# One core, hybrid attention with PEER: the program order of the attention stage written anew

## The chip, the cores and the metric

The kernel runs on one core of one Trainium2 chip. The metric is the device time of the whole program in microseconds (us); smaller is better. The engines are named as in the profile: PE (TensorE, its weight loads apart as PEld), DVE (VectorE), ACT (ScalarE), POOL (GpSimd), and SP, whose queue issues nearly all DMAs.

## The reference

One decoder layer over 512 tokens of width 1024, all in float32. Cut to what matters:

```
ada = silu(c) @ w_ada + b_ada            # six vectors: shift, scale, gate, twice
h = x*(1+scale1) + shift1
qa, ka, va, qb, kb, vb = split(h @ w_in)
oa = sliding-window attention (8 heads, 2 KV heads, window 128, ALiBi, sinks)
ob = stick-breaking attention (8 heads): A[t,s] = sigmoid(z_ts) * prod_{s<j<t}(1 - sigmoid(z_tj))
x = layer_norm(ALPHA*x + gate1 * (concat(rms(oa), rms(ob)) @ w_out))
h = x*(1+scale2) + shift2
x = layer_norm(ALPHA*x + gate2 * peer(h))  # product-key retrieval over 128*128 single-neuron experts
```

## The kernel before

The program has three stretches. The first stage (up to about 314 us) makes the modulation vectors, the projections, both attentions, the output projection and the first layer norm. The second scores the PEER keys and takes the best sixteen, the third streams all expert weights through PE. The change touches the first stage alone.

Every product of full precision is done in three matmuls: an operand is split into a rounded high part (`uhi`, `vwhi`, `hhi`, made by ACT, line 92) and the rest (`ulo`, `vwlo`, `hlo`, made by DVE or POOL, line 93). The stage is built from a few helpers that the program calls one after another:

- `proj_chunk(i, nm)`: 128 columns of the input projection (24 matmuls, line 303, into a PSUM tile `pj`). Chunks 0 to 7 are q and k of the four stick-breaking pairs, 8 is `ka`, 9 to 12 are `qa` of the four local pairs. The weights come by SP into `uraw` (two buffers).
- `proj_v(half)`: half of all V columns (96 matmuls, line 322). It needs three SBUF tiles of the tag `big`: the raw weights, their high and their low part. The tag has four buffers.
- `ada_rows(g, ...)` and `ada_cols(g)`: one of the modulation vectors. Four transfers of 1 MB (`wa`, tag `big` too) are summed by DVE in eight steps of 128x1024 (lines 170 and 172, `acc`); then PE reduces `acc` over the partitions (lines 189 and 179).
- `sb(j, q, k)`: the weights of one stick-breaking pair, two heads r after one another. For each head: scores `z` (line 367, one PSUM tile), three ACT steps (lines 370 to 372), DVE (374), POOL cuts the causal triangle (340 and 342), DVE (376, 377), the split into `sphi` and `splo`, fourteen matmuls that add the running sums (382, 384), ACT's exponential (387), and the cut once more. There is one `z`, so the next head's scores wait for this head's exponential.
- `sbv(j, w)`: the values of that pair (line 398), into the PSUM tile `oacc`, of which there is one; then `finish_o` copies it out on ACT (lines 349 and 352 or 355).
- `swa_pair(j, q, k)`: one local pair: scores `zs` (421), DVE (424 to 436), ACT's exponentials (431), transposes `pt` (451), copies `pts` (453) and values (456), into the same `oacc`. `zs` and `pt` share two PSUM buffers.

Tile names in the profile are those of the code. The code names no engine order for this stage: it is written in program order, a scheduler ahead of the run makes a fixed order for each engine from it, in which `sb` and `sbv` have high priority, and each engine then runs its own order strictly, waiting on semaphores. A tile whose buffer is still in use makes its writer wait. So the program order decides which rows stand behind which on each engine, and which transfer stands behind which on SP.

The other lines that the rows below name: 274 is the first part of chunks 0 to 3, 556 the output projection (`zm`), 521 the sums for the RMS norm, 502 the product of the output weights with `gate1`.

Of the kernel before, what the change touches and what calls it, by code (L numbers as in the profile page):

```python
# [67 lines left out]
def tile_block(ctx, tc, xr, xT, ccol, wada, bcol, brow, wqk, wv, sinks, gncol, wout,  # L68
# [73 lines left out]
    with ExitStack() as front:  # L142
# [32 lines left out]
        def ada_cols(g):  # L175
            acc = ada_acc(g)
            p = ps.tile([P, 512], F32, name="adap", tag="m", bufs=2)
            for dc in range(DC):
                T.matmul(p[:, dc:dc + 1], acc[:, dc * P:(dc + 1) * P], ones[:, 0:1], start=True, stop=True,
                         skip_group_check=True)  # L180
            V.tensor_tensor(adac[:, g * 8:g * 8 + 8], p[:, :DC], bc[:, g * 8:g * 8 + 8], op=OP.add)

        def ada_rows(g, dst, i):
            acc = ada_acc(g)
            bb = fa.tile([P, D], F32, name="bb", tag="big", bufs=BIG)
            nc.sync.dma_start(bb, brow[i:i + 1, :].to_broadcast([P, D]))
            for h in range(2):
                p = ps.tile([P, 512], F32, name="adap", tag="m", bufs=2)
                T.matmul(p, ones, acc[:, h * 512:(h + 1) * 512], start=True, stop=True)
                V.tensor_tensor(dst[:, h * 512:(h + 1) * 512], p, bb[:, h * 512:(h + 1) * 512], op=OP.add)  # L190

        def load_w_in(i):
            return load_split(wqk[i].rearrange("p (c n) -> p c n", c=DC), [P, DC, P], "u", wsp)
# [76 lines left out]
        def half_proj(i, h):  # L270
            (hi, lo), p = heads[i]
            for dc in range(*PARTS[h]):
                for n, (a, b) in enumerate(((hi, hhi), (hi, hlo), (lo, hhi))):
                    T.matmul(p, a[:, dc], b[:, dc], start=(dc == 0 and n == 0), stop=(dc == DC - 1 and n == 2))  # L274
# [19 lines left out]
        def proj_chunk(i, nm):  # L294
            if i < 4:
                half_proj(i, len(PARTS) - 1)
                p = heads[i][1]
            else:
                hi, lo = load_w_in(i)
                p = ps.tile([P, S], F32, name="pj", tag="m", bufs=2)  # L300
                for dc in range(DC):
                    for n, (a, b) in enumerate(((hi, hhi), (hi, hlo), (lo, hhi))):
                        T.matmul(p, a[:, dc], b[:, dc], start=(dc == 0 and n == 0), stop=(dc == DC - 1 and n == 2))  # L303
            o = fw.tile([P, S], F32, name=nm, tag=nm)
            A.activation(o, p, AF.Copy, scale=0.125 if nm[0] == "q" else 1.0)
            return o
# [3 lines left out]
        def proj_v(*halves):  # L310
            for half in halves:
                raw = fa.tile([P, DC, 320], F32, name="vwraw", tag="big", bufs=BIG)
                nc.sync.dma_start(raw, wv[:, half].rearrange("p (c n) -> p c n", c=DC))
                hi = fa.tile([P, DC, 320], F32R, name="vwhi", tag="big", bufs=BIG)
                lo = fa.tile([P, DC, 320], F32R, name="vwlo", tag="big", bufs=BIG)
                split(raw, hi, lo, V)
                for tb in range(TB):
                    p = ps.tile([P, S], F32, name="pj", tag="m", bufs=2)
                    t = slice(tb * P, (tb + 1) * P)
                    for dc in range(DC):  # L320
                        for n, (a, b) in enumerate(((hhi, hi), (hhi, lo), (hlo, hi))):
                            T.matmul(p[:, :320], a[:, dc, t], b[:, dc], start=(dc == 0 and n == 0),
                                     stop=(dc == DC - 1 and n == 2))
                    A.activation(vr[:, tb, half * 320:(half + 1) * 320], p[:, :320], AF.Copy)
# [136 lines left out]
        gate1 = fc.tile([P, D], F32, name="gate1")  # L461
        def sb(j, q, k):
            with tc.high_priority():
                return sb_weights(q, k)

        def sbv(j, w):
            with tc.high_priority():
                sb_values(j, w)

        w = sb(0, proj_chunk(0, "q"), proj_chunk(1, "k"))  # L470
        q0, k0 = proj_chunk(2, "q"), proj_chunk(3, "k")
        proj_v(1)
        qa = proj_chunk(9, "qa")
        ada_rows(5, gate2, 1)
        proj_v(0)
        sbv(0, w)
        w = sb(1, q0, k0)
        ada_rows(2, gate1, 0)
        q0, k0 = proj_chunk(4, "q"), proj_chunk(5, "k")
        sbv(1, w)  # L480
        ka = proj_chunk(8, "ka")
        w = sb(2, q0, k0)
        swa_pair(0, qa, ka)
        qa1 = proj_chunk(10, "qa")
        swa_pair(1, qa1, ka)
        q0, k0 = proj_chunk(6, "q"), proj_chunk(7, "k")
        ada_cols(3)
        sbv(2, w)
        ada_cols(4)
        w = sb(3, q0, k0)  # L490
        fa_cm.__exit__(None, None, None)
        fwo = front.enter_context(tc.tile_pool(name="fwo", bufs=1, side="right", reuse_waits="tile"))
        qa2 = proj_chunk(11, "qa")
        swa_pair(2, qa2, ka)
        sbv(3, w)
        qa3 = proj_chunk(12, "qa")
        wo = [None] * DC

# [678 lines left out]
```

## Time and profile before

| | us |
|---|---|
| median of 3 runs (lowest to highest) | 1596.53 (1594.99 to 1599.22) |
| the profiled execution, its own time | 1595.99 |
| its span in the trace | 1594.3 |
| PE busy | 1554.9 (98% of the span) |
| DVE busy | 1220.3 (77%) |
| ACT busy | 647.5 (41%) |
| POOL busy | 455.8 (29%) |

The span is what the trace covers; the execution's own time is 1.69 us longer. Matmuls are pipelined and their ends are modelled, so a PE shown as busy can still hide short waits.

### The profile page before, as it was taken

What the parts mean: (1) busy time and instruction counts of PE and PEld (TensorE: products, weight loads), DVE (VectorE), ACT (ScalarE), POOL (GpSimd) and SP (SyncE); (2) the same over time, 40 slices, a digit from 0 to 9 for tenths busy, and PEclk for the clock granted to TensorE, in tenths of its full rate; (3) what the DMA queues carried; (4) which work ended last, traced back from release to release, by engine and by line L of the source; (5) the groups of instructions that cost most, each with busy time, mean ns of one, the idle gap of its engine ahead of it and who ended that gap; (6) DMA issues with size and microseconds to landing.
All of it is one profiled execution on the core that took longest, in us unless ns stands there. A gap on an engine that the chain in (4) does not pass through costs nothing.

```text
span 1594.3 us, 21985 instructions
## 1 busy us (share of the span) xinstructions
PE 1554.9 (98%) x8109; PEld 1346.3 (84%) x8109; DVE 1220.3 (77%) x2351; ACT 647.5 (41%) x935; POOL 455.8 (29%) x410
## 2 busy tenths in 40 slices
PE   8999999999989999999999999999999999999996
PEld 5776767788879999899999999999999999998885
DVE  2568585589999997578777787777877777777878
ACT  2535574333355555333333333333333333333331
POOL 0002133544400000233334333333333444333100
PEclk8999898999999999999999999999999999999999
DMA  9564132222225555999888988999889998989873
GB/s 338 184 258 158 53 112 101 79 92 81 81 80 212 219 210 202 334 327 326 305 311 301 326 301 304 306 309 322 302 303 312 307 321 301 311 282 305 261 231 119
DMA packets 147356, 382.12 MB, mean 240 GB/s; under 512 B 11312, under 2 KB 68656, under 8 KB 143280
## 3 DMA queue, kind: packets, MB, share of 16 engines
q1 hardware_dynamic: 110384, 246.49, 44.6%
q0 software_dynamic: 36864, 134.23, 24.4%
q8 instruction: 63, 1.03, 0.3%
q14 instruction: 45, 0.37, 0.1%
HBM read 351.32 MB, written 29.36 MB: 239 GB/s over the span
## 4 chain that ended last, share of the span: by engine, by line
PE 79%; DVE 12%; DMA 3%; ACT 3%; issue 1%; POOL 1%; SPq 0%; DVEq 0%; ACTq 0%; POOLq 0%
PE yb L980 32%; PE ph L970 25%; PE pw L841 5%; PE ph L806 4%; PE pj L303 3%; PE zm L556 2%; DVE scr L620 1%; PE pj L274 1%; DMA wa<-in_wada_dram 1%; DVE tsi L622 1%; DVE tsi L619 1%; PE pq L647 1%; DVE tsv L621 1%; DVE tsv L618 1%; PE oacc L398 1%
## 5 line engine op out<-in xcount | busy, mean ns | idle before, releaser
L855 POOL DMA_INDIRECT gat<-in_u_rows_dram,idx x128 | 161.6, 1262 | 478.5 <-DVE hd L873 226.5
L93 DVE TENSOR_TENSOR ulo<-uraw,uhi 128x1024 fp32r<-128x1024 f32 x133 | 162.5, 1223 | 164.9 <-ACT uhi L92 160.5
L970 PE MATMUL ph<-h2hi,ulo 128*128 128x384 f32 x768 | 258.6, 337 | 0.6 <-DVE ulo L93 0.6
L970 PE MATMUL ph<-h2hi,uhi 128*128 128x384 f32 x768 | 258.2, 336 | 0.3 <-ACT uhi L92 0.3
L970 PE MATMUL ph<-h2lo,uhi 128*128 128x384 f32 x768 | 258.2, 336 | 0.0
L855 POOL DMA_INDIRECT gat<-in_v_rows_dram,idx x128 | 161.0, 1258 | 264.8 <-DVE y L883 224.1
L980 PE MATMUL yb<-vhi,ghi 128*128 128x512 f32 x654 | 203.0, 391 | 0.0
L980 PE MATMUL yb<-vhi,glo 128*128 128x512 f32 x654 | 202.9, 391 | 0.0
L980 PE MATMUL yb<-vlo,ghi 128*128 128x512 f32 x654 | 202.6, 391 | 0.0
L92 ACT ACTIVATE uhi<-uraw 128x1024 fp32r<-128x1024 f32 x155 | 162.4, 1050 | 74.6 <-PE pq L647 52.9
L883 DVE SCALAR_TENSOR_TENSOR y<-gat,cf,y 128x1024 f32<-128x1024 f32 x127 | 162.7, 1281 | 3.9 <-DMA gat<-in_v_rows_dram,idx 1.6
L873 DVE CUSTOM_DVE_ANT_0 gscr<-gat,h2row 128x1024 f32<-128x1024 f32 x128 | 156.5, 1222 | 10.6 <-DMA gat<-in_u_rows_dram,idx 7.9
L1085 ACT ACTIVATE stash<-ph 128x384 f32<-128x384 f32 x96 | 47.2, 491 | 275.1 <-PE ph L970 275.1
L970 PEld LDWEIGHTS ph<-h2lo,uhi 128*128 128x128 f32 x768 | 144.4, 188 | 4.4
L970 PEld LDWEIGHTS ph<-h2hi,uhi 128*128 128x128 f32 x768 | 144.4, 188 | 4.4 <-ACT uhi L92 0.7
L980 PEld LDWEIGHTS yb<-vlo,ghi 128*128 128x128 f32 x654 | 122.7, 188 | 27.3
L980 PEld LDWEIGHTS yb<-vhi,glo 128*128 128x128 f32 x654 | 122.8, 188 | 26.8
L970 PEld LDWEIGHTS ph<-h2hi,ulo 128*128 128x128 f32 x768 | 144.4, 188 | 1.0 <-DVE ulo L93 1.0
L980 PEld LDWEIGHTS yb<-vhi,ghi 128*128 128x128 f32 x654 | 121.8, 188 | 18.9
L93 DVE TENSOR_TENSOR vlo<-vraw,vhi 128x1024 fp32r<-128x1024 f32 x97 | 118.4, 1220 | 17.5 <-ACT vhi L92 17.4
L92 ACT ACTIVATE vhi<-vraw 128x1024 fp32r<-128x1024 f32 x97 | 102.8, 1060 | 53.6 <-issue 35.8
L947 ACT ACTIVATE ghi<-gt 128x384 fp32r<-128x384 f32 x97 | 51.0, 525 | 177.7 <-DVE gt L920 177.7
(311 smaller groups left out, 2860.1 us busy)
## 6 DMA issues: line engine op xcount, KB each, us to landing
uraw<-in_uT_dram SPq DMA_DIRECT2D x128, 512.0 KB, 5.2
vraw<-in_v_rows_dram SPq DMA_DIRECT2D x128, 512.0 KB, 5.2
w_d<-stage SPq DMA_DIRECT2D x12, 2048.0 KB, 7.3
wt<-w_d SPq DMA_DIRECT2D x32, 768.0 KB, 9.3
wa<-in_wada_dram SPq DMA_DIRECT2D x16, 1024.0 KB, 6.5
wah<-in_wada_dram SPq DMA_DIRECT2D x16, 512.0 KB, 9.4
uraw<-in_wq_dram SPq DMA_DIRECT2D x16, 512.0 KB, 3.3
uraw<-in_wqk_dram SPq DMA_DIRECT2D x11, 512.0 KB, 7.8
```

The lines of the kernel that those rows point to most:

```text
L92: A.activation(hi, src, AF.Copy)
L93: (eng or V).tensor_tensor(lo, src, hi.bitcast(F32), op=OP.subtract)
L303: T.matmul(p, a[:, dc], b[:, dc], start=(dc == 0 and n == 0), stop=(dc == DC - 1 and n == 2))
L806: T.matmul(p[:, :ND], a[:, dc], b[:, dc, P:], start=(dc == 0 and n == 0), stop=(dc == DC - 1 and n == 2))
L841: T.matmul(p[:, k * P:(k + 1) * P], oh4[:, 1, :, k], oh4[:, 2 + j, :, k], start=(j == 0), stop=(j == 1), skip_group_check=True)
L855: G.indirect_dma_start(out=t, out_offset=None, in_=rows, in_offset=bass.IndirectOffsetOnAxis(ap=idx[:, k:k + 1], axis=0))
L873: V.tensor_tensor_reduce(out=scr, in0=t, in1=h2row, scale=1.0, scalar=0.0, op0=OP.mult, op1=OP.add, accum_out=hd[:, n:n + 1])
L883: V.scalar_tensor_tensor(y0, t, cf[:, k:k + 1], y0, op0=OP.mult, op1=OP.add)
L947: A.activation(gop[i][0], gts[i], AF.Copy)
L970: T.matmul(p[:, :ND], a[:, dc], b[:, dc, P:], start=(dc == 0 and n == 0), stop=(dc == DC - 1 and n == 2))
L980: T.matmul(ybank[b][c0 // 512][:, c0 % 512:(c1 - 1) % 512 + 1], x[:, t], y[:, c0:c1], start=(i == 0 and n == 0), stop=(n == 2 and i == (NK ...
L1085: A.activation(stash[i + LOOK], p[:, :ND], AF.Gelu_apprx_tanh)
```

## The change

The calls of the attention are put in another order; nothing is computed otherwise, and no size or pool is altered. Both V halves now come directly behind the first pair's weights, the weights of stick-breaking pair j+1 directly behind the values of pair j, and the local pairs and the modulation vectors behind those.

```diff
         w = sb(0, proj_chunk(0, "q"), proj_chunk(1, "k"))
         q0, k0 = proj_chunk(2, "q"), proj_chunk(3, "k")
+        proj_v(0)
+        sbv(0, w)
+        w = sb(1, q0, k0)
         proj_v(1)
         qa = proj_chunk(9, "qa")
         ada_rows(5, gate2, 1)
-        proj_v(0)
-        sbv(0, w)
-        w = sb(1, q0, k0)
-        ada_rows(2, gate1, 0)
         q0, k0 = proj_chunk(4, "q"), proj_chunk(5, "k")
         sbv(1, w)
+        w = sb(2, q0, k0)
         ka = proj_chunk(8, "ka")
-        w = sb(2, q0, k0)
+        ada_rows(2, gate1, 0)
+        q0, k0 = proj_chunk(6, "q"), proj_chunk(7, "k")
+        sbv(2, w)
         swa_pair(0, qa, ka)
+        w = sb(3, q0, k0)
+        ada_cols(3)
         qa1 = proj_chunk(10, "qa")
+        sbv(3, w)
         swa_pair(1, qa1, ka)
-        q0, k0 = proj_chunk(6, "q"), proj_chunk(7, "k")
-        ada_cols(3)
-        sbv(2, w)
         ada_cols(4)
-        w = sb(3, q0, k0)
         fa_cm.__exit__(None, None, None)
         fwo = front.enter_context(tc.tile_pool(name="fwo", bufs=1, side="right", reuse_waits="tile"))
         qa2 = proj_chunk(11, "qa")
         swa_pair(2, qa2, ka)
-        sbv(3, w)
         qa3 = proj_chunk(12, "qa")
```

What this does to the engines' fixed orders is shown at three places. The first is DVE, from the split of the projection weights on, while the first stick-breaking pair's weights are made. Before:

```order
L93 TENSOR_TENSOR ulo<-uraw,uhi 128x1024 x2
L170 TENSOR_SCALAR acc<-wa,silu 128x1024
L172 SCALAR_TENSOR_TENSOR acc<-wa,silu,acc 128x1024
L374 SCALAR_TENSOR_TENSOR e<-z,e 128x1280
L172 SCALAR_TENSOR_TENSOR acc<-wa,silu,acc 128x1024
L376 COPY e<-e 128x128
L377 TENSOR_TENSOR e<-e 128x128
L172 SCALAR_TENSOR_TENSOR acc<-wa,silu,acc 128x1024
L93 TENSOR_TENSOR splo<-e,sphi 128x1536
L172 SCALAR_TENSOR_TENSOR acc<-wa,silu,acc 128x1024 x4
```

The same place now:

```order
L93 TENSOR_TENSOR ulo<-uraw,uhi 128x1024 x2
L374 SCALAR_TENSOR_TENSOR e<-z,e 128x1280
L376 COPY e<-e 128x128
L377 TENSOR_TENSOR e<-e 128x128
L93 TENSOR_TENSOR splo<-e,sphi 128x1536
L93 TENSOR_TENSOR vwlo<-vwraw,vwhi 128x2560
L374 SCALAR_TENSOR_TENSOR e<-z,e 128x1280
L376 COPY e<-e 128x128
L377 TENSOR_TENSOR e<-e 128x128
L170 TENSOR_SCALAR acc<-wa,silu 128x1024
L172 SCALAR_TENSOR_TENSOR acc<-wa,silu,acc 128x1024
L93 TENSOR_TENSOR splo<-e,sphi 128x1536
```

The steps of the first modulation vector have gone from the first head to behind the second, and the second V half's low part (the second `vwlo`) now stands between the two heads.

The second place is PE, at the scores of the second head. Before:

```order
L322 MATMUL pj<-vwhi,hlo 128x320
L322 MATMUL pj<-vwhi,hhi 128x320
L367 MATMUL z<-q,k 128x512
L367 MATMUL z<-q,k 128x384
L367 MATMUL z<-q,k 128x256
L367 MATMUL z<-q,k 128x128
L322 MATMUL pj<-vwlo,hhi 128x320
```

The same place now:

```order
L322 MATMUL pj<-vwhi,hhi 128x320
L322 MATMUL pj<-vwlo,hhi 128x320
L367 MATMUL z<-q,k 128x512
L398 MATMUL oacc<-e,vr 64x512
L367 MATMUL z<-q,k 128x384
L367 MATMUL z<-q,k 128x256
L367 MATMUL z<-q,k 128x128
L322 MATMUL pj<-vwhi,hlo 128x320
```

A matmul of the first head's values has moved in among the scores of the second. From this second `z` to the third, PE's order now holds 55 matmuls of line 322 (ten of the first V half, then the second half); before, it held twenty of line 322 and 24 of line 303.

The third place is PE at the end of the attention, from the values of the last pairs on. Before:

```order
L451 MATMUL pt<-ident,prs 128x128 x3
L556 MATMUL zm<-wohi_1722,hlo 128x512
L556 MATMUL zm<-wohi_1729,hhi 128x512 x2
L556 MATMUL zm<-wolo_1730,hhi 128x512 x2
L556 MATMUL zm<-wohi_1729,hlo 128x512 x2
L456 MATMUL oacc<-pts,vr 64x128
L451 MATMUL pt<-ident,prs 128x128 x7
L456 MATMUL oacc<-pts,vr 64x128 x7
L451 MATMUL pt<-ident,prs 128x128 x3
L456 MATMUL oacc<-pts,vr 64x128
```

The same place now:

```order
L456 MATMUL oacc<-pts,vr 64x128
L421 MATMUL zs<-ka,qa 128x128
L456 MATMUL oacc<-pts,vr 64x128 x5
L421 MATMUL zs<-ka,qa 128x256 x3
L421 MATMUL zs<-ka,qa 128x128
L421 MATMUL zs<-ka,qa 128x256 x3
L451 MATMUL pt<-ident,prs 128x128 x4
L456 MATMUL oacc<-pts,vr 64x128
L451 MATMUL pt<-ident,prs 128x128 x7
L456 MATMUL oacc<-pts,vr 64x128 x7
L451 MATMUL pt<-ident,prs 128x128 x3
L456 MATMUL oacc<-pts,vr 64x128
```

Before, the last local pair's scores stood ahead of the last stick-breaking values; now the last two local pairs stand one behind the other after them, and the last one has no row of other work among its own.

## Rows read from the trace of the kernel before

**Rows 1.** The page, part 4: the chain that ended last, shares by engine.

```profile
PE 79%; DVE 12%; DMA 3%; ACT 3%; issue 1%; POOL 1%; SPq 0%; DVEq 0%; ACTq 0%; POOLq 0%
```

**Rows 2.** Busy time by stretch: us, then each engine's busy us, granted clock, DMA share.

```profile
57.70:131.00 73.30, 72.21 (x371) 56.17 (x370) 54.10 (x48) 32.87 (x37) 8.97 (x12) 1.00 0.70 262
131.00:186.60 55.60, 54.34 (x281) 39.03 (x280) 39.23 (x94) 37.79 (x70) 12.86 (x21) 1.00 0.19 63
186.60:200.20 13.60, 13.60 (x54) 9.67 (x54) 4.33 (x6) 4.04 (x6) 1.27 (x1) 0.50 0.17 58
200.20:241.40 41.20, 37.91 (x190) 25.56 (x186) 35.61 (x81) 30.81 (x57) 15.88 (x17) 0.96 0.38 128
```

**Rows 3.** PE's waits, 57 to 255 us, one of them: total us, times, longest.

```profile
PE zm L556 <- POOL hlo L93: 1.6, 1, 1.6
```

**Rows 4.** PE in order of time, heads 0 to 2: start us, us, instruction.

```profile
58.03 2.42 PE L367 MATMUL z<-q,k 64*128 64x512 f32 x8
60.38 0.41 PE L322 MATMUL pj<-vwhi,hhi 128*128 128x320 f32 x1
...
69.66 0.84 PE L382 MATMUL z<-sphi,negtri 128*128 128x512 f32 x3
...
70.81 0.36 PE L322 MATMUL pj<-vwhi,hlo 128*128 128x320 f32 x1
...
74.22 2.42 PE L367 MATMUL z<-q,k 64*128 64x512 f32 x8
...
89.62 2.42 PE L367 MATMUL z<-q,k 64*128 64x512 f32 x8
```

**Rows 5.** DVE and POOL in order of time, heads 0 and 1.

```profile
57.36 2.82 DVE L93 TENSOR_TENSOR vwlo<-vwraw,vwhi 128x2560 fp32r<-128x2560 f32 x1 [3.99 <-ACT vwhi L92]
65.85 1.27 DVE L172 SCALAR_TENSOR_TENSOR acc<-wa,silu,acc 128x1024 f32<-128x1024 f32 x1
66.00 1.50 POOL L340 TENSOR_SCALAR_AFFINE_SELECT e<-e 128x384 f32<-128x384 f32 x1 [60.49 <-DVE e L374]
82.12 0.52 POOL L340 TENSOR_SCALAR_AFFINE_SELECT e<-e 128x384 f32<-128x384 f32 x1 [6.65 <-DVE e L374]
```

**Rows 6.** The chain in order of time, two of its pieces: start us, us.

```profile
110.44 1.98 PE adap L189 x4
112.43 8.32 PE pj L303 x35
```

**Rows 7.** ACT in order of time, behind a pair's values.

```profile
111.54 0.68 ACT L349 ACTIVATE oT<-oacc,gn 128x512 f32<-128x512 f32 x1
```

**Rows 8.** PE in order of time, around 186.6 us.

```profile
182.62 1.84 PE L179 MATMUL adap<-ones,acc 128*128 128x1 f32 x16
...
189.61 3.41 PE L179 MATMUL adap<-ones,acc 128*128 128x1 f32 x16
```

**Rows 9.** PE in order of time, the end of the attention.

```profile
233.50 1.78 PE L421 MATMUL zs<-ka,qa 64*128 64x128 f32 x8
238.67 2.77 PE L398 MATMUL oacc<-e,vr 128*64 128x384 f32 x9
246.35 0.98 PE L451 MATMUL pt<-ident,prs 128*128 128x128 f32 x7
247.80 1.09 PE L456 MATMUL oacc<-pts,vr 128*64 128x128 f32 x14 [0.47 <-ACT pts L453]
250.13 0.87 PE L456 MATMUL oacc<-pts,vr 128*64 128x128 f32 x10
```

**Rows 10.** Groups by line, 57 to 255 us: count, busy us, mean ns, idle before.

```profile
L431 ACT ACTIVATE prs<-prs,nm 128x256 f32<-128x256 f32 (+1 forms) x32 | 15.0, 472 | 5.3 <-DVE nm L427 5.3
L424 DVE CUSTOM_DVE_ANT_0 prs<-zs,bias,sink 128x256 f32<-128x256 f32 (+1 forms) x32 | 13.1, 445 | 8.2 <-PE zs L421 8.1
L436 DVE TENSOR_SCALAR prs<-prs,den 128x256 f32<-128x256 f32 (+1 forms) x32 | 10.6, 391 | 0.1
L453 ACT ACTIVATE pts<-pt 128x512 f32<-128x512 f32 (+1 forms) x16 | 8.7, 541 | 11.4 <-PE oacc L456 7.7 <-PE pt L451 3.5
```

## The prediction

> **What bounds the kernel now.** The page comes first: the chain that ended last is PE for 79% of the span [rows 1], so a microsecond that PE loses anywhere is, as a rule, a microsecond of the total. Then the busy times by stretch, cut where the change acts. From 57.7 us, where the second stretch of projections begins, to 241.4 us, where the last stick-breaking values end, PE is idle for only 1.09 us (73.30 less 72.21), then 1.26, 0 and 3.29 us [rows 2]. Two things beside that are to be seen there: from 186.6 to 200.2 us the granted clock is 0.50, the lower of TensorE's two levels (1.2 of 2.4 GHz), and DVE, ACT and POOL all have room. So this stage is bound by PE, waits little, and loses time mainly to its clock. No order of the calls can remove PE work. It can gain the waits and the low clock, and it can lose by leaving PE with nothing to do beside a stick-breaking head or a local pair.
>
> How long such a head takes is read from PE in order of time [rows 4]. The scores of heads 0, 1 and 2 begin at 58.03, 74.22 and 89.62 us: 16.2 and 15.4 us from one to the next, because there is one `z`. From a head's scores to its first running sum are 11.6 us (58.03 to 69.66), 9.3 of them behind the end of the scores (60.38). In that time PE lives on other work: 61 matmuls of line 322 fill it (60.38 to 69.66, 0.152 us each), those of line 303 take 0.238 us each (35 in 8.32) and the two reductions of a modulation vector 1.9 us [rows 6], and one set of running sums takes 1.15 us (69.66 to 70.81).
>
> **The change part by part.** The order alone moves; the counts of matmuls, DVE steps and transfers stay. The sum is made against the profiled execution's 1595.99 us, which is 0.54 us below the median of the runs.
>
> *The second V half right behind the first: +2.5.* The tag `big` has four buffers. The first half's raw, high and low parts and the second's raw part fill them; the second's high part takes the place of the first raw one, and its low part has to wait until the last matmul of the first half has read its buffer. Then DVE makes it in 2.82 us [rows 5]. PE's order holds two matmuls of the second half ahead of the first that reads the low part, 0.3 us. So PE stands for 2.82 - 0.3 = 2.5 us. Behind this DVE step the next head's step of line 374 is queued, and only the ACT steps of that head run meanwhile. Before, the second half was loaded only behind a modulation vector, and this step lay beside the projection of chunk 9. Bounds: nothing, if a buffer were free earlier, and 2.9 with the hand-over on top. I take 2.5, because the order leaves no other work there.
>
> *Heads one behind the other: +3.7.* I compare the chain with what PE's new order holds. Head 1 to head 2: the 55 matmuls of line 322 (8.4), scores (2.35), two sets of sums (2.3) and a first piece of the values (0.6) make 13.6 us against 15.4; the wait for the low V part lies in the same gap and fills it, so only the hand-over at the piece of values between the scores remains, about 0.2. Head 2 to head 3: behind the scores stand 51 matmuls of line 322 and one of line 303, 8.0 us, against 9.3; and ACT has the copy of the finished values (0.68 [rows 7]) and a square of about that size ahead of this head's second and third step. 1.3 + 2 x 0.68 would be 2.7; part of the copies fits ahead of the scores' end, so I take 2. Head 3: 26 of line 303 (6.2) and the two reductions of a modulation vector (1.9) against 9.3, uncovered 1.2. Head 4: 25 of line 303 (5.95) and two reductions (1.9), uncovered 1.4. Heads 5 to 7 have 30 projections or local rows beside them and are covered. Sum 0.2 + 2 + 1.2 + 1.4 = 4.8, less the 1.1 us of waits that the old order had in its first part [rows 2]: 3.7. Below it can be nothing, where a wait here only takes the place of a later one, and above 8, where also the transfers of 1 MB for the modulation vectors, whose DVE steps now stand ahead of the third and fourth heads' steps, come late.
>
> Here one contention enters. The cut on POOL took 1.50 us where DVE's step of line 172 ran beside it (65.85 and 66.00 us) and 0.52 us where DVE stood idle [rows 5]. In the new order of DVE no such step stands between line 374 and the copy behind the cut for the first heads, so I use the shorter chain of 15.4; with 16.2 the same gaps would cost 2.4 us more. The Trainium skill (SBUF — State Buffer, section "Who interferes with whom") says the same: a VectorE instruction with two SBUF inputs and a GpSimd instruction that reads SBUF block each other. The trace agrees, 1.50 against 0.52 us.
>
> *The end of the attention: +2.1.* The values of all pairs use one `oacc`, and scores and transposes of the local pairs share two buffers. So behind the last stick-breaking values now come, strictly in turn, the values of local pair 1, all of pair 2 and all of pair 3. One pair from its first scores to the next pair's: scores 0.45 (two of eight in 1.78 [rows 9]), four reductions on DVE 1.8, eight exponentials on ACT 3.8, scaling on DVE 1.6, four transposes 0.56, copy 0.54, values 0.55, two more copies 1.1 [rows 9, 10], and about 0.6 for small steps: 11 us. Until pair 2's scores 2.7 us pass (copy 0.68, values 0.7, two copies 1.1, hand-overs). The last values then end 2.7 + 11 + 11.5 = 25.2 us behind the stick-breaking ones; before, it was 9.6 us (241.44 to 251.00 [rows 9]). In return PE has this work no longer ahead of them: scores of two pairs (32 in 7.1), transposes of one (14 in 2.0), values of two (56 in 4.4), 13.5 us. So 25.2 - 9.6 - 13.5 = 2.1. With a turn of 9 us instead of 11 the term is -1.9, with 13 us 6.1.
>
> *What goes.* The wait of 1.6 us of the output projection for POOL's low part [rows 3]: in the new order that POOL work stands between the last head's two cuts, while PE still has projections. -1.6; if it comes back, 0.
>
> *The clock: 0.* Sixteen one-column matmuls took 1.84 us at the upper level and 3.41 at the lower [rows 8]; at that ratio the 13.6 us at the lower level cost 6.3. What ran ahead of the fall were local pairs' small matmuls, one-column reductions and scores, without a wait. The new order has the same kinds of rows in a similar row, so the likeliest is that the loss stays. Bounds: -6.3 and, below, +6.
>
> Sum: 2.5 + 3.7 + 2.1 - 1.6 + 0 = +6.7, which gives 1602.7 us. SP's queue moves too (the first modulation vector's transfers go behind both V halves and four chunks of weights), but each chunk's weights still stand ahead of their use by more than the longest of these waits, so I cost that at nothing; uncovered, one late chunk would cost what a head's gap does, 2 us.
>
> **The rivals.** *The clock does not fall.* The reductions of the modulation vectors are now spread over four places instead of two near each other. For it: no wait preceded the fall, so it hangs on the mix of rows. Against it: the mix of local rows remains. 1602.7 - 6.3 = 1596.4.
>
> *Faster: the stage runs at PE's own work.* If early heads only put the waiting where PE had waited anyway, the stage gains its waits of 5.6 us and the clock's 6.3, 11.9 in all, and ends at 1584.1; with half of it at 1590. For it: heads finished early free the output projection's first matmuls. Against it: the end of the attention, which now has no other rows. It decides from where all new waits together stay under 7.1 us (11.9 less 4.8).
>
> *Slower: the clock falls more.* Two pairs in turn leave PE busy for a small part of 25 us, and each new gap is a place where the clock may go to its lower level; the PE pieces in the two turns (about 3 us) would double and another stretch like rows 2's would cost 6. About 1610. It decides if a stretch at 0.50 appears that has no counterpart before. The Trainium skill (TensorE: Matmul & The Clock Gate, "HAM oscillation") holds that idle gaps between bursts bring the clock down; by that rule this rival would be the likeliest. The trace does not bear it out: the fall at 186.6 us followed a stretch with 1.26 us of idle in 55.6.
>
> **How the numbers follow.** A measurement of this kernel can tell about 0.3%, 4.8 us, from no change. The forecast (own range 1598 to 1608) has 0.50, the clock that stays up 0.20, the faster rival 0.18, the slower one 0.12. Slower by over 0.3%: 0.42 of the forecast and 0.12, so 0.54. Within: 0.08 of the forecast, 0.16 of the second case, 0.03 of the third, 0.27. Faster: 0.19. For 8 in 10 the range runs from 1590 (half of the faster rival's gain) to 1611.
>
> **What would show it.** Right: a wait of PE of 2.5 us at line 322 for DVE's `vwlo` near 81 us; scores of heads 1, 2 and 3 about 17 to 20 us apart; some 25 us from the last values of line 398 to the last of line 456; the first `zm` of the second token block some 7 us later than before. Wrong: the V wait absent, the heads' sums without waits, a granted clock of 1.00 from 131 us on, or a turn of a local pair under 9 us.

## The result, and the profile after

The changed kernel takes 1610.71 us (median of 4 runs, 1608.76 to 1614.15). The kernel before, on the same chip, takes 1597.88 (1594.99 to 1599.82). The ratio is 1.0085, 95% interval 1.0070 to 1.0100: 12.8 us slower. The forecast was slower, at 1602.7, with a range of 1590 to 1611: the direction holds, the range by 0.3 us, and the size is about half of what came. The profiled execution is one of 1608.76 us, its span 1607.0, 12.7 more than before.

The page's part 4 reads as it did [rows 1], so PE's lost microseconds are still the kernel's:

```profile
PE 80%; DVE 12%; ACT 3%; DMA 2%; SPq 1%; issue 1%; POOL 0%; DVEq 0%; ACTq 0%; POOLq 0%
```

The busy times by stretch (us, then each engine's busy us, granted clock, DMA share), in the cuts of [rows 2] up to 200.2 us. There I cut anew: 228.06 us is now the end of the last stick-breaking values (241.44 before), 267.49 the first `ssp`, the reduction behind the attention (253.62 before).

```profile
57.70:131.00 73.30, 68.69 (x352) 54.04 (x352) 46.07 (x43) 35.48 (x36) 9.89 (x16) 0.98 0.54 194
131.00:186.60 55.60, 55.06 (x238) 38.69 (x235) 38.97 (x64) 28.08 (x43) 10.19 (x15) 0.97 0.39 142
186.60:200.20 13.60, 13.56 (x89) 9.79 (x87) 9.52 (x20) 9.74 (x14) 2.22 (x4) 1.00 0.25 79
200.20:228.06 27.86, 23.99 (x104) 16.39 (x103) 24.81 (x39) 18.18 (x36) 17.57 (x13) 0.89 0.36 114
228.06:267.49 39.43, 32.66 (x172) 21.84 (x172) 15.86 (x69) 20.13 (x58) 7.87 (x9) 0.82 0.15 54
```

Three things are to be seen. In the first stretch PE is idle for 4.61 us, where it was 1.09. From 186.6 to 200.2 us the clock is at 1.00, where it was 0.50. And a stretch of 39.43 us now stands between the last stick-breaking values and `ssp`, with 6.77 us of idle and a clock of 0.82; before it was 12.18 us long (241.44 to 253.62), at a clock of 1.00:

```profile
241.44:253.62 12.18, 11.15 (x68) 7.84 (x69) 2.27 (x7) 7.39 (x19) 3.83 (x3) 1.00 0.01 3
```

From `ssp` on the two run nearly alike: it comes 13.9 us later, the first `zt` 12.9 (280.48 against 267.57), the end of the span 12.7. So all of the loss lies ahead of `ssp`, and more than all of it behind the last stick-breaking values: these end 13.4 us sooner, just the 13.5 us of work that was moved behind them, and the rest takes 27.3 us longer. One thing here is not the change's: the first head's scores began at 55.85 us in this execution and at 58.03 in that of before, and in the traces of all kernels below they begin between 55.85 and 58.24, whatever the order. From these scores to `ssp` the two traces differ by 16.0 us.

PE's waits from 57 to 270 us (total us, times, longest):

```profile
PE pt L451 <- DVE prs L436: 3.8, 2, 2.4
PE oacc L398 <- POOL e L340: 3.3, 3, 2.6
PE oacc L456 <- ACT pts L453: 2.2, 4, 1.0
PE pj L322 <- ACT vr L324: 1.8, 2, 1.1
PE zm L556 <- POOL hlo L93: 1.2, 1, 1.2
PE pj L322 <- DVE vwlo L93: 1.1, 1, 1.1
...
PE z L382 <- ACT sphi L92: 0.3, 1, 0.3
```

The second V half's low part is waited for 1.1 us (at 81.19 us), not 2.5, but the copies of V by ACT add 1.8 that were not forecast. The wait for POOL's low part [rows 3] has not gone. The waits at the heads' running sums, which the forecast priced highest in the early part, come to 0.3 us (line 382). The longest are new: transposes that wait for DVE's probabilities, in the turns of the local pairs.

PE in order of time at the end of the attention (start us, us, instruction, and in brackets the idle time before it and what ended it); before, these were [rows 9]:

```profile
223.53 4.53 PE L398 MATMUL oacc<-e,vr 128*64 128x512 f32 x14 [2.62 <-POOL e L340]
...
232.10 0.49 PE L421 MATMUL zs<-ka,qa 64*128 64x128 f32 x2
...
240.86 1.01 PE L451 MATMUL pt<-ident,prs 128*128 128x128 f32 x4 [1.39 <-DVE prs L436]
...
245.28 1.97 PE L456 MATMUL oacc<-pts,vr 128*64 128x128 f32 x14 [0.26 <-ACT pts L453]
...
248.63 0.66 PE L421 MATMUL zs<-ka,qa 64*128 64x128 f32 x2
...
256.07 1.16 PE L451 MATMUL pt<-ident,prs 128*128 128x128 f32 x4 [2.38 <-DVE prs L436]
...
263.99 0.87 PE L456 MATMUL oacc<-pts,vr 128*64 128x128 f32 x10
...
267.49 1.95 PE L521 MATMUL ssp<-ones,sqa 128*128 128x1 f32 x16 [0.56 <-POOL sqa L356]
```

The last stick-breaking values end at 228.06 us. Pair 2's scores begin at 232.10, pair 3's at 248.63 (16.5 us later), and pair 3's last values end at 264.86 (16.2 us after that). From the stick-breaking values to the end are 36.8 us; the forecast had 2.7 + 11 + 11.5 = 25.2. The pieces on PE are themselves slower: fourteen matmuls of line 456 take 1.97 us, 1.09 in [rows 9], so they ran at the lower of TensorE's two levels. Three stretches of the tail stood at that level (granted clock third from the end):

```profile
221.80:228.60 6.80, 5.07 (x16) 2.86 (x17) 3.98 (x3) 0.51 (x1) 2.90 (x3) 0.50 0.65 184
242.20:249.00 6.80, 6.09 (x29) 4.37 (x30) 1.36 (x6) 1.97 (x4) 0.00 (x0) 0.50 0.01 2
255.80:262.60 6.80, 5.31 (x27) 3.90 (x27) 2.42 (x11) 3.05 (x12) 0.00 (x0) 0.50 0.27 110
```

DVE in the same turns:

```profile
234.05 0.35 DVE L424 CUSTOM_DVE_ANT_0 prs<-zs,bias,sink 128x128 f32<-128x128 f32 x1 [6.18 <-PE zs L421]
...
242.56 1.07 DVE L436 TENSOR_SCALAR prs<-prs,den 128x128 f32<-128x128 f32 x4
```

From pair 2's first scores (232.10) to the end of its second head's scaling (242.56 and 1.07) are 11.5 us. The forecast had added up 8.2 us for this part of a turn (scores, reductions, exponentials, scaling, small steps). Transposes, copies and values, two rounds for each pair, then take up to 250.09: 6.5 us against 2.8.

### The profile page after: what moved, and what is told of

Read it like the earlier page. It is cut to its first block, busy times and chain, and to the rows that moved or that the text cites. A ratio compares the mean times of both kernels' runs of the same rounds, so it can differ in the third digit from the quotient of the medians.

```text
span 1607.0 us, 21976 instructions
## 1 busy us (share of the span) xinstructions
PE 1558.8 (97%) x8109; PEld 1346.9 (84%) x8109; DVE 1221.6 (76%) x2351; ACT 647.8 (40%) x935; POOL 461.4 (29%) x410
## 4 chain that ended last, share of the span: by engine, by line
PE 80%; DVE 12%; ACT 3%; DMA 2%; SPq 1%; issue 1%; POOL 0%; DVEq 0%; ACTq 0%; POOLq 0%
PE yb L980 32%; PE ph L970 25%; PE pw L841 5%; PE ph L806 4%; PE pj L303 2%; PE zm L556 2%; PE pj L322 2%; DVE scr L620 1%; PE z L367 1%; PE oacc L398 1%; DVE tsi L622 1%; DVE tsi L619 1%; DMA wah<-in_wada_dram 1%; PE pq L647 1%; PE zs L421 1%; PE oacc L456 1%
## 5 line engine op out<-in xcount | busy, mean ns | idle before, releaser
L873 DVE CUSTOM_DVE_ANT_0 gscr<-gat,h2row 128x1024 f32<-128x1024 f32 x128 | 156.4, 1222 | 10.7 <-DMA gat<-in_u_rows_dram,idx 8.2
L980 PEld LDWEIGHTS yb<-vlo,ghi 128*128 128x128 f32 x654 | 122.7, 188 | 27.3
```

The lines of the kernel that those rows point to most:

```text
L873: V.tensor_tensor_reduce(out=scr, in0=t, in1=h2row, scale=1.0, scalar=0.0, op0=OP.mult, op1=OP.add, accum_out=hd[:, n:n + 1])
L980: T.matmul(ybank[b][c0 // 512][:, c0 % 512:(c1 - 1) % 512 + 1], x[:, t], y[:, c0:c1], start=(i == 0 and n == 0), stop=(n == 2 and i == (NK ...
```

## The experiments

**What each tells apart.** Theory A was that the loss is the tail's, B that it is the early part's, C that the low clock only moves about. From here on "tail" means the time from the scores of the last stick-breaking head (its `z`) to `ssp`. Times are medians of 5 to 12 runs, and each ratio is to the kernel before on the same chip; it weighs all runs, and so is not just the quotient of the medians. The experiments ran on several chips, on which the kernel before has medians from 1597.27 to 1598.91 us, so two of them compared by their medians can differ by 1.6 us for that alone. "The changed kernel" is its 1610.71 us.

**1. Last values behind pair 2 again.**

```diff
-        sbv(3, w)
         swa_pair(1, qa1, ka)
...
         swa_pair(2, qa2, ka)
+        sbv(3, w)
```

> The changed kernel, with one line put back: the last stick-breaking head's values stand behind local pair 2 again, so that one local pair, not two, has nothing but itself at the end. Theory A (the tail): the last local values came 35.5 us behind the last stick-breaking values, 9.6 before, and 13.5 us of that is work that was only moved, so 12.4 us are lost in the turns of the two pairs; with one pair moved back most of it returns: about 1598 to 1601 us. Theory B (the early part: the second V half's wait and the heads one behind the other): the tail is no dearer than elsewhere, 1608 to 1611. Theory C (the low clock is a fixed amount that only moves): the tail's loss goes, but a stretch at the lower level comes back near 190 us, about 1604.

Measured: 1600.94 us, ratio 1.0026 (1.0013 to 1.0039). So 9.8 us come back from this one line, and what stays, 3.3 us (by the interval 2.1 to 6.2), is the price of the rest of the change. Theory A holds (its 35.5 us are the 36.8 read above); C does not: the clock near 190 us stays at 1.00 here as well. The tail, by one window (width, then PE's busy us first, granted clock third from the end), is first that of the changed kernel, then of this one:

```profile
199.36:267.49 68.13, 57.49 (x276) 38.51 (x276) 41.51 (x113) 39.15 (x94) 25.85 (x22) 0.85 0.24 81
```

```profile
200.68:256.21 55.53, 50.67 (x276) 34.83 (x276) 41.59 (x113) 38.95 (x94) 18.67 (x22) 0.94 0.28 100
```

12.6 us shorter, of which idle gives 5.8 (10.64 less 4.86), and most of the rest is the lower clock, which costs 8.2 us in the one and 3.1 in the other.

**2. The new tail alone on the kernel before.** The last head's weights and values ahead of local pairs 1 and 2; all else as before. It is not quite the changed kernel's tail: there a reduction and a query projection stand between these weights and these values, here nothing does.

```diff
-        swa_pair(1, qa1, ka)
...
         sbv(2, w)
-        ada_cols(4)
         w = sb(3, q0, k0)
+        sbv(3, w)
+        swa_pair(1, qa1, ka)
+        ada_cols(4)
...
         swa_pair(2, qa2, ka)
-        sbv(3, w)
```

> The kernel before, with the end of the changed one alone: last stick-breaking values ahead of local pairs 1 and 2, V halves and first heads as before. Theory A: the two turns cost their 12.4 us here too, and the low clock near 190 us stays as before: 1608 to 1611 us. Theory B: what was forecast for the end, about 2 us: 1599 to 1601. Theory C: about 1604, the clock's fall near 190 us gone and the tail paid.

Measured: 1623.84 us, ratio 1.0150 (1.0133 to 1.0166). None of the three: 26 us by the medians, 24.0 by the ratio (21.2 to 26.5), twice the whole change. The tail's window, and two of PE's waits:

```profile
214.29:278.88 64.59, 46.77 (x206) 29.73 (x205) 26.86 (x79) 28.44 (x65) 14.82 (x16) 0.71 0.17 57
```

```profile
PE z L382 <- ACT sphi L92: 5.3, 1, 5.3
PE pt L451 <- DVE prs L436: 4.4, 2, 2.4
```

The tail is about as long as the changed kernel's (64.59 against 68.13), but PE has only 46.77 us of work in it, much of that at the lower level (clock 0.71). The last head itself now stands bare: PE waits 5.3 us for its `sphi`.

**3. V halves late, all else changed.** `proj_v(1)` stands first again, `proj_v(0)`, `sbv(0)` and `sb(1)` behind `qa` and the gate's rows.

> The changed kernel with the two V halves where the kernel before has them (second half ahead of the first, gate rows between); heads and tail as changed. Theory A: only the V wait of 1.1 us and the waits for V's copies of 1.8 us can go: 1607 to 1611 us. Theory B: the early part is what costs, so 1600 to 1605.

Measured: 1620.91 us, ratio 1.0160 (1.0139 to 1.0181), 10.2 us slower than the changed kernel by the medians, 12.0 by the ratios (these five runs lie 9.6 us apart). Neither theory: V early is a gain in the new order, not a cost.

```profile
210.38:273.94 63.56, 47.78 (x220) 31.27 (x221) 27.23 (x96) 32.17 (x83) 12.24 (x17) 0.73 0.15 50
```

The last projection (line 303) ends at 196 us here and at 218 in the changed kernel: V's matmuls, late, leave their place among the early heads to projections, and these are then missing in the tail.

**4. V late and last values behind pair 2.** Experiment 1 with the V halves late.

> The changed kernel with the V halves late, as before, and with the last stick-breaking values behind local pair 2, as before: only the heads' own order is new. With the new tail the late V halves cost 10 us more than the early ones (1620.9 against 1610.7). Theory A (parts add up): they cost the same 10 here, 1609 to 1612 us. Theory D (late V halves use up the projections that would cover the last head, and that costs only where no local pair covers it): 1601 to 1605.

Measured: 1611.63 us, ratio 1.0078 (1.0064 to 1.0092). Theory A's number; D, which wanted 1601 to 1605, falls in this form. With experiments 1 and 3 it makes a square:

| us | last values behind pair 2 | ahead of pair 2 (as changed) |
|---|---|---|
| V early (as changed) | 1600.9 | 1610.7 |
| V late | 1611.6 | 1620.9 |

In the new order of heads the tail costs 9.8 or 9.3 us, and late V halves 10.7 or 10.2, whatever the other does; by the ratios it is 9.4 or 13.1, and 8.3 or 12.0, so that the two add is shown to some 4 us only. Here too the tail holds little work:

```profile
214.94:267.92 52.98, 41.06 (x220) 28.08 (x220) 28.63 (x96) 32.15 (x83) 11.35 (x17) 0.84 0.18 60
```

**5. V halves early, alone, on the kernel before.** `proj_v(0)`, `sbv(0)`, `sb(1)` ahead of `proj_v(1)`; the rest as before.

> The kernel before with only the V halves and the first head's values early, as in the changed kernel; later heads and the tail as before. Theory A (parts add up as forecast): the wait of PE for the second half's low part and V's copies, 1 to 3 us: 1598.5 to 1600.5. Theory D (early V saves projection work for the last heads, which matters only where the tail is bare): no gain here, 1597 to 1600, and the fall of the clock near 190 us may move by up to 6 us either way.

Measured: 1611.60 us, ratio 1.0081 (1.0067 to 1.0095). Neither: 12.7 us slower, with a tail as before (39.46 us). The loss shows in other places: the same waits for V as in the changed kernel (1.1 and 1.8 us), a wait for the sum of a modulation vector (`acc`) and stretches at the lower level:

```profile
PE adap L189 <- DVE acc L172: 3.3, 1, 3.3
```

```profile
120.00:140.00 20.00, 15.73 (x56) 9.62 (x55) 15.37 (x16) 6.64 (x8) 3.45 (x5) 0.83 0.80 282
204.00:214.00 10.00, 10.00 (x22) 6.74 (x22) 4.46 (x5) 4.72 (x4) 0.00 (x0) 0.50 0.36 105
```

So early V alone costs 12.7, the rest of the new order with neither early V nor the new tail (experiment 4) 12.7, and both together 3.3.

**6. Filler in the two turns.** 34 matmuls of ones by ones into free banks, their results not used, offered to PE beside pairs 2 and 3.

```diff
+        def fill(n):
+            zf = ps.tile([P, 1536], F32, name="zf", tag="z", bufs=1)
+            for i in range(n):
+                T.matmul(zf[:, 512 * (i % 3):512 * (i % 3) + P], ones, ones, start=True, stop=True, skip_group_check=True)
...
+            if j > 1:
+                fill((4, 14)[j - 2])
...
+                if j > 1 and n0 == 0:
+                    fill((8, 8)[j - 2])
```

> The changed kernel with 34 small extra matmuls (128x128, operands of ones, results not used) offered to the two last turns, where PE otherwise waits for DVE and ACT. They fill pair 2's turn, and output projection matmuls that had stood there come in pair 3's turn. Theory A1 (a turn takes 15.2 us because PE's pieces in it run at a granted clock of 0.6 to 0.7): the clock stays near 1.00, a turn falls to 11 or 12 us, the total to 1602 to 1605 us. Theory A2 (a turn is the latency of DVE's and ACT's steps, whatever PE's clock): the clock rises but the turn stays near 15, 1609 to 1612.

Measured: 1609.87 us, ratio 1.0076 (1.0062 to 1.0090), not to be told from the changed kernel. The clock did what it was to do: the row below begins at the end of the last stick-breaking values.

```profile
230.29:266.32 36.03, 34.98 (x238) 26.13 (x237) 16.47 (x70) 20.16 (x58) 7.86 (x9) 1.00 0.17 63
```

```profile
234.11 0.48 PE L421 MATMUL zs<-ka,qa 64*128 64x128 f32 x2
...
243.10 0.82 PE L458 MATMUL pt<-ident,prs 128*128 128x128 f32 x4
...
248.87 0.48 PE L421 MATMUL zs<-ka,qa 64*128 64x128 f32 x2
...
256.77 0.27 PE L458 MATMUL pt<-ident,prs 128*128 128x128 f32 x1
...
262.83 0.87 PE L465 MATMUL oacc<-pts,vr 128*64 128x128 f32 x10
```

With a clock of 1.00 from there to `ssp`, pair 2's scores and pair 3's are 14.8 us apart (234.11 to 248.87; 16.5 in the changed kernel), and pair 3's end comes 14.8 us later (263.70; 16.2). So the clock is worth 1.4 to 1.8 us of a turn, and 14.8 us are its steps. Theory A2 holds, A1 only for that small part. The total alone could not show it: from the first head's scores to `ssp` idle time fell by 5.3 us against the changed kernel and the cost of the lower clock by 5.0, but the fillers added 8.0 us to PE's work. That it is not the fillers which keep the turns long is seen in experiment 8, where at a clock of 1.00 and without them the turns take 15.9 and 14.7 us.

**7. Pair 3's scores in banks of their own.** They use the three banks of `z`, free by then, instead of the two shared with pair 2's transposes.

```diff
+        own = ps.tile([P, 1536], F32, name="zo", tag="z", bufs=1) if j == 3 else None
...
+            b = 512 * ((2 * r + qh) % 3)
+            z = own[:, b:b + 512].rearrange("p (a b) -> p a b", a=2)
```

> The changed kernel, but local pair 3 computes its scores in the three PSUM banks that the stick-breaking scores leave free, instead of the two banks it shares with pair 2's transposes. Its scores and the DVE and ACT steps on them can then run beside pair 2's turn. Theory A2 (a turn is the latency of its steps, one behind the other through two shared banks): the 6 us between pair 3's scores (250.0 us) and its first transpose (256.1) leave the path, 1603 to 1606 us. Theory A1 (a turn is long because PE is at its lower clock): the steps only change places, 1608 to 1611.

Measured: 1610.09 us, ratio 1.0073 (1.0059 to 1.0087). By the total, A1's number. By the trace the turn is shorter all the same:

```profile
243.63 1.01 PE L456 MATMUL pt<-ident,prs 128*128 128x128 f32 x4 [0.68 <-DVE prs L440]
...
254.81 0.98 PE L456 MATMUL pt<-ident,prs 128*128 128x128 f32 x4 [1.97 <-DVE prs L440]
...
262.89 0.87 PE L461 MATMUL oacc<-pts,vr 128*64 128x128 f32 x10
```

Pair 2's first transposes and pair 3's are 11.2 us apart, 15.2 in the changed kernel (240.86 to 256.07). Part of this may be the clock: here it was at 1.00 throughout,

```profile
243.63:254.81 11.18, 8.34 (x55) 5.26 (x55) 6.89 (x33) 7.52 (x26) 1.49 (x2) 1.00 0.08 18
```

and there at 0.50 for 6.8 us. With shared banks and a clock of 1.00 the same two are 13.7 us apart in experiment 6 (243.10 to 256.77) and 15.2 in experiment 8 below (235.70 to 250.91), so banks of their own are worth 2.5 to 4.0 us. The end comes 33.2 us behind the stick-breaking values (230.58 to 263.76) instead of 36.8. PE stays idle for 9.3 us of the tail (64.51 less 55.25):

```profile
201.88:266.39 64.51, 55.25 (x276) 36.66 (x276) 41.95 (x113) 39.04 (x94) 25.84 (x22) 0.89 0.25 86
```

Of the 3.6 us the medians show 0.6, which the runs can't tell from 3.6 or nothing. The two traces show where the rest went: from the first head's scores to `ssp` it is 3.5 us shorter than in the changed kernel (208.2 against 211.6), but these scores began 2.4 us later in this execution, and the part behind `ssp` took 2.5 us longer. The same edit on experiment 1's kernel made it slower:

> The first experiment's kernel (last stick-breaking values behind local pair 2) with pair 3's scores in banks of their own. Theory A2: pair 3's turn, the one turn left at the end, begins sooner, 2 to 5 us less than the 1600.9 of the first experiment: 1596 to 1599. Theory A1: 1600 to 1602.

Measured: 1605.63 us, ratio 1.0042 (1.0028 to 1.0055), against 1600.94 without it: neither theory's number. There pair 3's scores stand among pair 2's rows, the last stick-breaking values behind them end at 242.52 us instead of 240.49, and the tail grows from 55.5 to 58.7 us. Shared banks are thus one of the chain's links, and taking them away does not by itself pay.

**8. Work held back for the tail.** Pair 3's query projection (24 matmuls) accumulates in `z`'s banks, and so can't run until these are free.

```diff
+        if late:
+            p = ps.tile([P, 1536], F32, name="pz", tag="z", bufs=1)[:, :S]
+        else:
             p = ps.tile([P, S], F32, name="pj", tag="m", bufs=2)
...
-        qa3 = proj_chunk(12, "qa")
+        qa3 = proj_chunk(12, "qa", late=True)
```

> The changed kernel, but pair 3's query projection (24 matmuls, about 5.6 us of PE) accumulates in the banks that the last stick-breaking scores leave, so it can't run before they are free: it moves from beside the last head into pair 2's turn, and the output projection's matmuls that stood there into pair 3's. No work is added or left out. Theory D (the loss is PE waiting in the turns while it had covering work to spare before): the last head's values end about 5 us sooner, the turns are filled, the total falls by 4 to 7: 1604 to 1607 us. Theory A2 (turns take what they take and the head before them too): 1609 to 1612.

Measured: 1605.16 us, ratio 1.0047 (1.0031 to 1.0063): 5.5 us less than the changed kernel, in the middle of what D expected. Behind the stick-breaking values:

```profile
223.31:260.29 36.98, 33.97 (x200) 23.04 (x199) 19.44 (x72) 22.60 (x63) 11.66 (x12) 1.00 0.25 86
```

```profile
227.11 0.48 PE L424 MATMUL zs<-ka,qa 64*128 64x128 f32 x2
...
243.01 0.49 PE L424 MATMUL zs<-ka,qa 64*128 64x128 f32 x2
...
256.80 0.87 PE L459 MATMUL oacc<-pts,vr 128*64 128x128 f32 x10
```

The last values end 22.4 us behind their head's scores (200.89 to 223.31; 28.7 in the changed kernel). Behind them PE is busy for 33.97 of 36.98 us at a clock of 1.00. The turns are little shorter (15.9 and 14.7 us against 16.5 and 16.2); they have work beside them. From the first head's scores to `ssp` idle time fell by 3.1 us and the cost of the lower clock by 4.6. On experiment 1's kernel the same edit did harm:

> The first experiment's kernel (last stick-breaking values behind local pair 2) with pair 3's query projection held back in the same way. Theory D: there the tail had 4.9 us of idle and 3.1 us lost to the clock, of which half could be covered: 1596 to 1600 us, at or below the kernel before. Theory A2: 1600 to 1603.

Measured: 1604.39 us, ratio 1.0041 (1.0028 to 1.0054), 3.5 us slower than experiment 1 and above both ranges. The last values end at 246.19 us there, at 240.49 without it: in PE's fixed row they stand behind pair 2's transposes, which now come late.

```profile
235.52 1.11 PE L454 MATMUL pt<-ident,prs 128*128 128x128 f32 x4 [0.59 <-DVE prs L439]
...
243.82 2.37 PE L401 MATMUL oacc<-e,vr 128*64 128x512 f32 x16
```

So held work helps only where it stands behind nothing that others wait for.

**9. The early falls of the clock.** In [rows 8] sixteen one-column matmuls ran 4 us ahead of the fall at 186.6. First one such group was moved (`ada_cols(3)` to behind `ka`), on the kernel before.

> The kernel before with the modulation reduction of group 3 moved ahead, so that its eight one-column matmuls no longer stand within a few rows of group 4's, ahead of the clock's fall at 186.6 us; all else as before. If that cluster brought the clock down (the second case of the forecast: the clock does not fall where the reductions are spread), the 6.3 us come back: 1591 to 1594. If the fall hangs on the local pairs' rows there: 1597 to 1600.

Measured: 1599.22 us, ratio 1.0005 (0.9996 to 1.0014). The total says "the local pairs' rows"; the trace says otherwise. In the execution that was profiled, the fall near 187 us is gone, and one of the same length begins 3 us behind the start of the moved group (this execution, of 1595.95 us, was the shortest of the eleven, so the median is not its number):

```profile
135.55 1.84 PE L179 MATMUL adap<-ones,acc 128*128 128x1 f32 x16
```

```profile
138.60:152.20 13.60, 13.60 (x36) 9.77 (x36) 8.28 (x30) 4.87 (x13) 2.43 (x4) 0.50 0.11 39
186.60:200.20 13.60, 13.60 (x85) 9.91 (x85) 6.56 (x6) 5.82 (x9) 1.85 (x3) 1.00 0.35 116
```

Then the reductions were given 64 columns instead of one; the 63 others are not read.

```diff
-                T.matmul(p[:, dc:dc + 1], acc[:, dc * P:(dc + 1) * P], ones[:, 0:1], start=True, stop=True,
+                T.matmul(p[:, 64 * dc:64 * dc + 64], acc[:, dc * P:(dc + 1) * P], ones[:, :64], start=True, stop=True,
```

> The kernel before, with the two column reductions of the modulation (groups 3 and 4) done as 64-column instead of one-column matmuls; the 63 other columns are not read. Theory E (a group of one-column matmuls brings the clock to its lower level some 3 us later: in nine of thirteen such groups in the traces a stretch at 0.50 began 2 to 5 us behind): the stretch from 187 to 201 us is gone and 4 to 6 us come back, 1592 to 1595 us. Rival (the fall hangs on the local pairs' rows beside them): 1596 to 1600.

Measured: 1590.54 us, ratio 0.9967 (0.9950 to 0.9984): 6.7 us faster than the kernel before by the medians (by the ratio 5.3, 2.6 to 8.0), more than theory E expected, and the fastest of all. The stretch of [rows 2] that stood at 0.50:

```profile
186.60:200.20 13.60, 13.60 (x81) 9.82 (x79) 7.22 (x7) 10.70 (x15) 3.30 (x3) 1.00 0.25 77
```

```profile
181.40 1.89 PE L179 MATMUL adap<-ones,acc 128*128 128x64 f32 x16
```

The stretch at 0.50 is gone, at no cost (1.89 us for the sixteen, 1.84 with one column). PE's order shifted by some rows as well, so not all of the 6.7 need be the clock's. That time goes with the clock can be seen in the kernel before itself: of its 27 executions on this chip the longest took 1602.11 us at a mean granted clock of 0.981 and the shortest 1590.56 at 0.990, while the ten with wide reductions ran at 0.987 to 0.990. On the changed kernel:

> The changed kernel with the same 64-column reductions. Theory E: only the short fall near 170 us goes, worth about 2 us, and the tail's falls stay, since no reduction stands there: 1607 to 1611 us. If the tail's falls are of the same kind as the early ones and go too: 1602 to 1605.

Measured: 1606.99 us, ratio 1.0061 (1.0039 to 1.0083), 3.7 us less than without (the two intervals overlap), at the lower edge of what theory E expected. The short fall near 170 us is gone, and the tail's remain. With the projection held back as well:

> The changed kernel with pair 3's query projection held back for the tail and the 64-column reductions. Theory E with D: falls at 170 and 190 us go, 3 us less than the 1605.2 of the held projection alone: 1600 to 1603 us. If the two do not add up: 1604 to 1607.

Measured: 1603.13 us, ratio 1.0036 (1.0021 to 1.0051), 2 us less than experiment 8, not told apart from it. And on experiment 1's kernel:

> The first experiment's kernel (last stick-breaking values behind local pair 2) with the 64-column reductions. Theory E: the short fall near 173 us goes, 1.5 to 2 us less than 1600.9: 1598 to 1600. Rival: 1600 to 1603.

Measured: 1600.17 us, ratio 1.0021 (1.0009 to 1.0034), the same as without.

## Why the forecast had the sign and not the size

The time from the first head's scores to `ssp` was split for each kernel into PE's idle time, what the lower level cost (busy time by one less the granted clock), and the rest, PE's work, which is 180 to 185 us in all of these kernels. From before to changed the three grew by 9.1, 2.8 and 4.1 us; what the 4.1 consist of no run shows. The first two, added over 40 windows of each trace, and the tail's length:

| kernel | against before, us | idle | lower clock | tail, us |
|---|---|---|---|---|
| before | 0 | 6.7 | 8.3 | 36.8 |
| changed | +12.8 | 15.8 | 11.1 | 68.1 |
| 1: values behind pair 2 | +3.3 | 10.1 | 6.1 | 55.5 |
| 2: new tail alone | +26.2 | 19.9 | 18.2 | 64.6 |
| 3: V late | +23.3 | 20.3 | 13.7 | 63.6 |
| 4: V late, values behind pair 2 | +12.7 | 14.7 | 15.3 | 53.0 |
| 5: V early alone | +12.7 | 13.7 | 11.0 | 39.5 |
| 8: projection held back | +7.4 | 12.7 | 6.5 | 59.4 |
| 9: wide reductions on before | -6.7 | 6.1 | 1.4 | 36.3 |

The tail is a chain of steps whose length follows from what stands in it: 36 to 40 us with heads and tail in the order of before, 53 to 56 with the new heads and all of pair 2 between the last head's scores and its values, 64 to 68 with two pairs behind the values. It is no constant: the held-back projection brought the changed kernel's to 59.4, and experiment 1's kernel has 59.3 with wide reductions. Where PE has that much work left it is covered; where the projections are used up it is not, and the gap is idle time and low clock.

*The end of the attention: +2.1.* This is the step that failed. Against experiment 1 it costs 9.8 us. The forecast allowed that with a turn of 13 us instead of 11 the term would be 6.1; the turns took 16.5 and 16.2. What was mis-sized is the turn: I had added the durations of its steps and put next to nothing for what lies between them. Scores fill two banks, DVE empties them, the next scores follow, and the second head's probabilities are done 11.5 us behind the first scores instead of 8.2; each of the two rounds of transpose, copy and values waits again. At the upper level a turn is still 14.8 us (experiment 6). Sharing two banks makes 2.5 us or more of the 3.8 above 11 (experiment 7); the rest was not taken apart. The lower level adds 1.4 to 1.8. The 9.8 us hold beside the new order of heads; beside the old one a similar tail cost 24 to 26 (experiment 2).

*Second V half: +2.5, and heads one behind the other: +3.7, less 1.6.* Together +4.6; experiment 1 measures +3.3 (2.1 to 6.2) for them. The sum is about right by luck, its parts are not. The V wait is 1.1 us and the copies of V 1.8. The heads' scores came 17.3, 18.3 and 19.7 us apart, as forecast (17 to 20), but not for the reason given: the waits at the running sums, most of the 3.7, came to 0.3, and heads' sums without waits were one of the forecast's own signs of being wrong. Behind the waits for V the clock was at 0.50 from 81.8 to 85.2 us, which was not forecast. The POOL wait stayed, so nothing went. Above all these are not terms that can be added: either one alone costs 12.7.

*The clock: 0.* Up to the last head's scores it costs 3.4 us instead of 6.8, in the tail 8.2 instead of 1.7 (in windows of 1 us, finer than the table's). The second case, that the clock does not fall, is half right: the long fall went (a short one near 170 us took its place), and experiment 9 shows that it follows the one-column reductions, which I had named as what is spread. Its 6.3 us did not reach the total.

*The rival "slower: the clock falls more", about 1610.* It had the time and the stretches at 0.50 in the turns. Its mechanism is the smaller part of the turns: they took 32.7 us together where the forecast had 22.5, and with the clock at 1.00 they were 3.2 shorter (experiment 6). The Trainium skill (TensorE: Matmul & The Clock Gate, "HAM oscillation") holds that idle gaps between bursts bring the clock down. I said that the trace did not bear that out; for the tail it does: the clock was at 1.00 until the waits of 2.62 us (ended 223.53), of 1.39 and 0.77 us (ended 240.86 and 242.65) and of 2.38 us (ended 256.07), and at 0.50 from 221.8, 242.2 and 255.8 us, each time for 6.8 us. The trace of before had such a fall too, which I passed over: at 238.0 us, for 3.4 us, behind a wait of 1.68 us that ended at 237.38. For the falls at 186.6 us before and at 138.6 us in experiment 9 it does not: these followed a PE that hardly waited.

*The rival "faster: the stage runs at PE's own work".* The new waits did not stay under 7.1 us: idle time alone grew by 9.1.

What stays open is why V early alone leaves 7.0 us more idle time and 2.7 more at the lower clock than before, with a tail as short as before, and why these go when the heads' order changes too.

## What to carry to other kernels

Price a turn of dependent steps from one turn seen in a trace, from its first instruction to the next turn's first, and not as a sum of durations: what lay between the steps, the alternation through two shared buffers among it, made 14.8 us out of 11. When calls are reordered on a bound engine, ask first how much free work is left beside the last chain; held-back work gave 5.5 us of 12.8 back here, where it stood behind nothing that others wait for. But do not add up the prices of single moves: two that each cost 12.7 us cost 3.3 together. Low clock beside idle time may be only its companion: fill the gaps and time it before calling it the cause, and count what the filler itself takes.

## What the runs showed of the hardware

One-column reductions of a modulation vector, on a PE that hardly waited, stood 2 to 5 us ahead of a stretch at the lower level in 16 of 23 places in the traces of before, after and experiments 1 to 8 and the first of 9; groups that began at the lower level are not counted. (Theory E's nine of thirteen counted fewer of them.) The stretches lasted 3.4 to 13.6 us. The first group of a trace was followed by one in all thirteen traces, the second in three of ten; why the others differ is open. With 64 columns none of eight groups was, in four traces; sixteen such matmuls took 0.05 us more, and the kernel before became 6.7 us faster.

One more group of one-column matmuls was left as it was in every run, the sums for the RMS norm (`ssp`, line 521, sixteen). In 15 of 17 traces a stretch at the lower level began 1.4 to 4.5 us behind its start, at 255.0 us in the trace of before. PE had waited for up to 0.6 us just ahead of it, and no run widened it, so whether it is the cause is not shown.
